# A hybrid decoder layer on one core: split gates in four chunks, and a bank of its own for each product of the second in-projection

## The chip, the cores and the metric

The kernel runs on one core of one Trainium2 chip. The metric is device microseconds (us) of one execution. Five engines matter: TensorE (PE: matmuls; PEld is its weight load), VectorE (DVE), ScalarE (ACT), GpSimd (POOL) and SyncE (SP), which issues most transfers. Results of matmuls land in PSUM, which this program divides into eight banks of 128 partitions x 512 fp32 numbers, and ACT or VectorE carries them from there to SBUF.

## The reference

One layer of a decoder over 2048 positions with 1024 features, all in float32:

```python
h = rms_norm(x, norm1_g)
z = h @ w_in                                   # 1024 -> 2*1024 + 3*512
lru_x, lru_gate, sc_b, sc_c, sc_x = split(z)
lru_x = causal_dwconv(lru_x, lru_conv_w) + lru_conv_b
y_lru = rg_lru(lru_x, ...) * gelu(lru_gate)
y_sc = sc_b * causal_dwconv(sc_c * sc_x, sc_conv_w)
x = x + concat(y_lru, y_sc) @ w_out            # 1536 -> 1024
h = rms_norm(x, norm2_g)
gate, up = split(causal_dwconv(h @ w_up, ffn_conv_w))
x = x + (gelu(gate) * up) @ w_down             # 3072 -> 1024
return rms_norm(x, final_g)
```

`rg_lru` is a gated linear recurrence over positions. Its two gates are `sigmoid(lru_x @ wa + ba)` and `sigmoid(lru_x @ wx + bx)`, where `wa` and `wx` hold 16 blocks of 64x64 on the diagonal. From the gates come a decay `a` and an input `b`, and `h[t] = a[t] h[t-1] + b[t]`.

## The kernel before

Features lie on the partitions, positions along the free axis. The 2048 positions are worked on in two halves of T = 1024, and a half in two blocks of NB = 512, one PSUM bank each. A matmul in the fast form reads operands that are rounded (fp32r). To keep the accuracy of fp32, each operand is split in a high part (ACT copies and rounds, line 239) and a low part (VectorE subtracts, line 240), and a product is made of three matmuls: high x high, high x low, low x high. Where operands are left in plain fp32, one matmul is written, which the trace shows as two records.

The stages follow each other on PE: the in-projection of the first half (0 to about 290 us, `in_phase`), the out-projection of the first half (to about 440), the in-projection of the second half (`in_blocks`, to about 742), its out-projection (to about 860), then the two halves of the ConvFFN.

*First in-projection.* The operands of x are made chunk by chunk (`x_prep`: xh on ACT, line 463, xl on VectorE, line 464); beside that the squares of x are taken on ACT (line 309) and added up on VectorE in ss_a (line 310). The sum is split into rh_a and rl_a, and PE multiplies both with ones to get the mean (ms_a, line 327). After that come the units one by one: eight chunks L0 to L7 of the recurrence and four of the short convolution. For each L chunk `lru_gates` (line 380) makes four plain fp32 matmuls, two blocks times two row halves of 64 partitions, where the row halves are the two 64x64 blocks of the chunk. gw holds the gate weights, cv the convolved input.

*Second in-projection.* Two output chunks at a time, a pair, are made for both blocks by Strassen's scheme in Winograd's form: seven products in place of eight, of four contraction steps each, 12 matmuls per product. W11, W12, W22 are weights as they are loaded, S1 to S4 sums of them; the sums were made in the first half and stored. There are 14 pairs: L0 to L7, three of kind B (the factor sc_b) and four of kind X. A weight operand wW or wS of 128x512 is loaded by SP in pairs (line 842; the name wr_in8W_8W tells that both belong to pair 8) and split into high and low on ACT and VectorE.

For a pair, PE runs W11, then S2, S3 and W22 in one chain in the same bank (zx). After each of them the bank's running sum is wanted, so ACT copies it to SBUF (line 700) before PE goes on in it. S1 and S4 share the bank zc, and W12 has za; these are added to the copies by VectorE (line 704). A round on PE holds the first products of pair j and the last ones of pair j-1, and between them the gates of an earlier chunk. The first output of a pair is called xlin for kind L, prin for X and sbin for B, the second one soin.

When a pair of kind L is complete, `finish` makes its convolution (line 354 on ACT, line 356 on VectorE, three steps), and a round later come the gates, eight sigmoids on ACT (line 391) and the rest of the recurrence with the scan (line 404). Beside all this, the mean of squares for the next norm is gathered: sx_b is squared on ACT (line 1188) and added to ss_b on VectorE (line 1189).

*What sets the order.* PE, SP and GpSimd work in the order in which the program is written. On ACT and VectorE a scheduler places the instructions; a block under `tc.high_priority(offset=...)` ranks ahead by that offset. Each engine then works strictly in the order placed. Pools limit how far it can go ahead: eight banks, two pages for the loads of weights, six for their parts.

Of the kernel before, what the change touches and what calls it, by code (L numbers as in the profile page):

```python
# [12 lines left out]
P = 128  # L13
# [18 lines left out]
GP = 0  # L32
UPP = 200
CP = 160
LATE = ("11", "22")
HSIDE = 1
LASTA = NLRU - 1
# [62 lines left out]
def block_kernel(  # L100
# [275 lines left out]
    def lru_gates(c, half, cv, gw):  # L376
# [3 lines left out]
                nc.tensor.matmul(ps[t], gw[rows, :], cv[rows, blk(t)], start=True, stop=True)  # L380
        return pss

    def lru_scan(c, half, cv, g, *gates, home=None, sign=1.0):
        n = f"{half}_{c}"
        r, i = (flat(p(f"{x}{n}")) for p, x in zip(home or (act, act), "ri"))
# [105 lines left out]
    def in_phase(half, acc, between):  # L491
# [19 lines left out]
            if k == 2:  # L511
                nc.sync.dma_start(prm, par[:, KC:])
        for k in range(KC):
            x_square(half, k, acc, xs[k])
        for _ in loads[2]:
            pass
        gate_w.append(flat(tmp("gw")).rearrange("p (c k) -> p c k", c=NLRU))
        nc.sync.dma_start(gate_w[0], w_gate.rearrange("c p k -> p c k"))
        parts = mean_split(acc, f"a{half}")
        pair_sums(0, NLRU)  # L520
        rs = inv_rms(acc, f"a{half}", parts)
        nc.gpsimd.tensor_copy(mark, rs[:, 0:1])
        ready.append(True)
        ps_2 = pss[2]
        for k in range(2, KC):
            product_step(ps_2, wcol(wts[2], k), acts[k], False, k == KC - 1)
        sum_step()
        cv = lru_conv(0, half, pss[0], rs)
# [3 lines left out]
        for n, (kind, c) in enumerate(UNITS):  # L532
            nxt = UNITS[n + 1] if n + 1 < len(UNITS) else None
            if kind == "L":
                if len(cur) < 2:
                    cur = (*cur, lru_gate(c, half, in_product(NLRU + c, half, acts), rs))
                cv, g = cur
                ps_n = ps_2 or in_product(first_product(nxt), half, acts)
                ps_2 = None
                ps_g = in_product(NLRU + nxt[1], half, acts) if n == 0 else None  # L540
                gates = lru_gates(c, half, cv, gate_w[0][:, c, :])
                if nxt[0] == "L":
                    cur = (lru_conv(nxt[1], half, ps_n, rs),)
                    if ps_g is not None:
                        cur = (*cur, lru_gate(nxt[1], half, ps_g, rs))
                y = lru_scan(c, half, cv, g, *gates)
            else:
                y = sc_second(c, half, acts, rs, sc_first(c, half, acts, rs, ps_n))
                if nxt is not None:
                    ps_n = in_product(first_product(nxt), half, acts)  # L550
                    if nxt[0] == "L":
                        cur = (lru_conv(nxt[1], half, ps_n, rs),)
            keep_y(half, n, y, (4, 8) if n >= NOUT - 2 else (7, 7))
            between(n)
# [123 lines left out]
    class Pair:  # L678
# [17 lines left out]
                    )  # L696

        def copy(self, dst):
            with tc.high_priority(offset=HP):
                nc.scalar.activation(dst, self.x, AF.Copy)  # L700

        def add(self, dst, ps):
            with tc.high_priority(offset=HP):
                nc.vector.tensor_tensor(dst, ps, dst, ALU.add)

        def spread(self):
# [125 lines left out]
    def in_weights(ops):  # L832
# [11 lines left out]
        for at, (i, op) in enumerate(ops):  # L844
            home = vpage if early else raw_tile
            t = home(f"w{op}_in{i}")
            split(t[:, 0, :], t[:, 1, :], raw[:, at, :])
            out.append((t[:, 0, :], t[:, 1, :]))
        return out

# [3 lines left out]
    class InPair(Pair):  # L854
# [5 lines left out]
        def open(self):  # L860
# [7 lines left out]
            else:  # L868
                self.first = flat(vpage(f"sb{n}"))
                self.g = halves(self.first, 0)  # L870

        def first_term(self):
            self.begin()

        def second_term(self):
            self.second()

        def third_term(self):
            self.sum1()

        def fourth_term(self):
            self.run(self.x, "S2", "T2", False, False)
            self.copy(self.g[1])

        def fifth_term(self):
            self.run(self.x, "S3", "T3", False, False)
            self.open_second()
            self.copy(self.n[1])
            self.add(self.n[1], self.c)

        def sixth_term(self):
            self.end()

        def seventh_term(self):
            self.fourth()

        def open_second(self):
            self.other = flat(vpage(f"so{self.name}"))
# [498 lines left out]
```

## Time and profile before

| | us |
|---|---|
| median of 3 runs (2258.54 to 2259.25) | 2259.07 |
| the profiled execution | 2254.52 |
| its span in the trace | 2252.5 |

The granted clock of the profiled execution is 0.998 of full speed. The trace is of one execution of its own; its span goes from the first instruction to the last. The page gives busy times per engine, the idle time of each engine with what ended it (the releaser), and a chain followed back from the last instruction. An engine that waits for another is named in the list of waits as "PE zxin L689 <- ACT soin L700": PE's instruction that writes zxin, at line 689, waited for ACT's instruction that writes soin, at line 700.

### The profile page before, as it was taken

To read this page: it belongs to the slowest core of one execution; us is meant where nothing else is said; L and a number is where in the kernel's file an instruction comes from. 1 tells how busy PE (TensorE), PEld (TensorE's weight loads), DVE (VectorE), ACT (ScalarE), POOL (GpSimd) and SP (SyncE) were. 2 spreads that over 40 slices of the span, in tenths; PEclk is the share of its full clock that TensorE was granted. 3 is DMA by queue.
4 is the path that set the end of the run, shared out by engine and by line. 5 is a ranking of instruction groups with operands and counts; after the bars stand their busy time and mean duration, and the time that the engine had idled before them with its cause. 6 is when DMAs were issued, how large, how long until landed. Compare 5 with 4: busy or idle time off the path is not lost.

```text
span 2252.5 us, 26402 instructions
## 1 busy us (share of the span) xinstructions
PE 2223.2 (99%) x9754; PEld 1815.1 (81%) x9754; DVE 1780.7 (79%) x2062; ACT 1216.2 (54%) x1411; POOL 175.7 (8%) x302
## 2 busy tenths in 40 slices
PE   9999999999999899999999999999999999999997
PEld 7887788887767688888888788888888888888886
DVE  8767879847778899898887887676988888886556
ACT  7538835557797554555544454444544444453343
POOL 0021110000000000110111100000000000000000
PEclk9999999999999999999999999999999999999999
DMA  8486369734434874565557477674223232359754
GB/s 313 104 236 187 121 227 303 273 108 136 164 121 128 311 267 169 180 195 173 166 164 222 128 254 243 232 254 137 99 100 111 98 113 90 108 196 346 243 193 156
DMA packets 157953, 415.01 MB, mean 184 GB/s; under 512 B 16640, under 2 KB 19328, under 8 KB 157248
## 3 DMA queue, kind: packets, MB, share of 16 engines
q1 hardware_dynamic: 135872, 354.86, 45.5%
q0 software_dynamic: 21808, 58.47, 10.1%
q8 instruction: 76, 1.25, 0.2%
q14 instruction: 53, 0.43, 0.1%
q10 hardware_dynamic: 144, 0.00, 0.0%
HBM read 311.55 MB, written 139.46 MB: 200 GB/s over the span
## 4 chain that ended last, share of the span: by engine, by line
PE 85%; issue 5%; ACT 4%; DVE 3%; DMA 2%; POOL 0%; SPq 0%; DVEq 0%; ACTq 0%; POOLq 0%
PE zx L689 21%; PE zin_b L295 13%; PE dx L1022 12%; PE zc L689 11%; PE dy L1022 9%; PE ox L1022 5%; PE za L689 5%; PE oy L1022 4%; PE zxin L689 2%; PE zS L689 1%; PE zcin L689 1%; PE zr_b L380 1%; PE zW L689 1%; PE zain L689 1%; ACT wS_in L239 0%
## 5 line engine op out<-in xcount | busy, mean ns | idle before, releaser
L239 ACT ACTIVATE fh_d<-wrf_d 128x1024 fp32r<-128x1024 f32 x84 | 89.0, 1060 | 204.3 <-PE dy L1022 78.4
L240 DVE TENSOR_TENSOR fl_d<-wrf_d,fh_d 128x1024 fp32r<-128x1024 f32 x84 | 102.7, 1223 | 120.7 <-ACT fh_d L239 118.4
L1022 PE MATMUL dx<-fh_d,wl_d 128*128 128x512 f32 x384 | 149.4, 389 | 0.0
L1022 PE MATMUL dx<-fh_d,wh_d 128*128 128x512 f32 x384 | 149.4, 389 | 0.0
L1022 PE MATMUL dx<-fl_d,wh_d 128*128 128x512 f32 x384 | 149.4, 389 | 0.0
L295 PE MATMUL zin_b<-xh,wh_in 128*128 128x512 f32 x448 | 139.4, 392 | 0.2
L295 PE MATMUL zin_b<-xl,wh_in 128*128 128x512 f32 x448 | 138.2, 389 | 0.1
L295 PE MATMUL zin_b<-xh,wl_in 128*128 128x512 f32 x448 | 137.9, 389 | 0.0
L240 DVE TENSOR_TENSOR wla_up<-wra_up,wha_up 128x1024 fp32r<-128x1024 f32 x48 | 58.8, 1224 | 98.3 <-ACT wha_up L239 98.3
L356 DVE SCALAR_TENSOR_TENSOR cg<-ug,prm,cg 128x1024 f32<-128x1024 f32 x96 | 122.8, 1279 | 8.1 <-ACT cg L352 7.3
L356 DVE SCALAR_TENSOR_TENSOR cu<-un,prm,cu 128x1024 f32<-128x1024 f32 x96 | 122.7, 1278 | 4.7 <-ACT cu L352 4.3
L689 PE MATMUL zc<-hhB,whd_up 128*128 128x512 f32 x368 | 120.8, 389 | 0.0
L689 PE MATMUL zx<-ht,whc_up 128*128 128x512 f32 x368 | 113.4, 389 | 0.0
L1022 PE MATMUL dy<-fh_d,wh_d 128*128 128x512 f32 x288 | 112.0, 389 | 0.0
L1022 PE MATMUL dy<-fl_d,wh_d 128*128 128x512 f32 x288 | 112.0, 389 | 0.0
L1022 PE MATMUL dy<-fh_d,wl_d 128*128 128x512 f32 x288 | 112.0, 389 | 0.0
L240 DVE TENSOR_TENSOR wl_d<-wrw_d,wh_d 128x1024 fp32r<-128x1024 f32 x84 | 102.3, 1218 | 8.3 <-ACT wh_d L239 7.0
L700 ACT ACTIVATE ug<-zx 128x512 f32<-128x512 f32 x92 | 54.8, 596 | 98.1 <-PE zx L689 93.1
L295 PEld LDWEIGHTS zin_b<-xh,wh_in 128*128 128x128 f32 x448 | 83.5, 188 | 23.7 <-issue 3.8
L295 PEld LDWEIGHTS zin_b<-xl,wh_in 128*128 128x128 f32 x448 | 84.1, 188 | 18.1 <-DVE xl L464 0.6
L295 PEld LDWEIGHTS zin_b<-xh,wl_in 128*128 128x128 f32 x448 | 84.1, 188 | 17.4
L239 ACT ACTIVATE wh_d<-wrw_d 128x1024 fp32r<-128x1024 f32 x84 | 87.8, 1046 | 11.6 <-PE zc L689 4.0
(552 smaller groups left out, 6332.2 us busy)
## 6 DMA issues: line engine op xcount, KB each, us to landing
wrc_up<-in_w_up SPq DMA_DIRECT2D x48, 512.0 KB, 4.9
f_d_T<-cg SPq DMA_DIRECT2D x96, 256.0 KB, 2.5
wrw_d<-sd_d_S SPq DMA_DIRECT2D x48, 512.0 KB, 4.6
wrf_d<-f_d_T SPq DMA_DIRECT2D x48, 512.0 KB, 4.2
f_d_B<-cu SPq DMA_DIRECT2D x72, 256.0 KB, 2.4
wrw_d<-in_w_down SPq DMA_DIRECT2D x36, 512.0 KB, 4.8
wrf_d<-f_d_B SPq DMA_DIRECT2D x36, 512.0 KB, 3.3
wr_in<-in_w_in SPq DMA_DIRECT2D x25, 512.0 KB, 5.9
```

Of the source, the lines that this page charges most:

```text
L239: nc.scalar.activation(r32(hi), src, AF.Copy)
L240: nc.vector.tensor_tensor(r32(lo), src, hi, ALU.subtract)
L295: nc.tensor.matmul(ps[t], r32(a), r32(b[:, blk(t)]), start=(first and i == 0), stop=(last and i == 2))
L356: nc.vector.scalar_tensor_tensor(dst, src[:, k : k + T], col(o_w + k), dst, ALU.mult, ALU.add)
L380: nc.tensor.matmul(ps[t], gw[rows, :], cv[rows, blk(t)], start=True, stop=True)
L689: nc.tensor.matmul(ps, r32(p[:, s]), r32(self.hs[k][x][o]), start=f and i == 0, stop=l and i == 2, skip_group_check=True,)
L700: nc.scalar.activation(dst, self.x, AF.Copy)
L1022: nc.tensor.matmul(ps[m], r32(p), r32(x[:, k, :]), start=first and i == 0 and n == 0, stop=(last or not on_x) and i == ni - 1 and n == 2, ...
```

## The change

There are three groups of edits. First, for chunks 2 to 5 of the first half the gates are made of split operands: cv is split in ch and cl, the gate weights of these four chunks are split once, and three products take the place of the one in fp32. This makes 12 matmuls of 64 rows in place of four. Second, in the second in-projection only W11 is still copied by ACT; W12, S2, S3 and W22 each get a bank of their own, and VectorE adds each to the sum in SBUF. The final values are the same sums in another order of work. Third, ranks: the copy of W11 gets 200 (was 120), the squares of x are raised by 20, the splits of weights in `in_weights` by 100. MK is 0, so that loop makes nothing.

```diff
--- before.py
+++ after.py
@@ -32,6 +32,15 @@
 GP = 0
 UPP = 200
 CP = 160
+MK = 0
+XP = 200
+AP = 120
+QP = 20
+IWQ = 100
+APART = ("S2", "S3", "W22")
+LAST_X = "W11"
+GQ = 60
+PARTS = (2, 3, 4, 5)
 LATE = ("11", "22")
 HSIDE = 1
 LASTA = NLRU - 1
@@ -380,6 +389,30 @@
                 nc.tensor.matmul(ps[t], gw[rows, :], cv[rows, blk(t)], start=True, stop=True)
         return pss
 
+    def lru_gates_of_parts(c, half, cv, gw):
+        pss = [pst2(f"z{name}{half}_{c}") for name in "ri"]
+        hi, lo = (flat(act(f"c{x}{half}_{c}")) for x in "hl")
+        with tc.high_priority(offset=GQ):
+            split(hi, lo, cv)
+        for i, (a, b) in enumerate(((gw[0], hi), (gw[0], lo), (gw[1], hi))):
+            for t in range(T // NB):
+                for ps, rows in zip(pss, HALVES):
+                    nc.tensor.matmul(ps[t], r32(a[rows, :]), r32(b[rows, blk(t)]), start=i == 0, stop=i == 2)
+        return pss
+
+    gate_parts = []
+
+    def gates_of(c, half, cv):
+        if c not in PARTS:
+            return lru_gates(c, half, cv, gate_w[0][:, c, :])
+        if not gate_parts:
+            n = max(PARTS) + 1 - min(PARTS)
+            t = flat(tmp("gp"))
+            for i in range(2):
+                gate_parts.append(t[:, i * n * P // 1 : (i + 1) * n * P].rearrange("p (c k) -> p c k", c=n))
+            split(*gate_parts, gate_w[0][:, min(PARTS) : max(PARTS) + 1, :])
+        return lru_gates_of_parts(c, half, cv, [g[:, c - min(PARTS), :] for g in gate_parts])
+
     def lru_scan(c, half, cv, g, *gates, home=None, sign=1.0):
         n = f"{half}_{c}"
         r, i = (flat(p(f"{x}{n}")) for p, x in zip(home or (act, act), "ri"))
@@ -511,18 +544,21 @@
             if k == 2:
                 nc.sync.dma_start(prm, par[:, KC:])
         for k in range(KC):
-            x_square(half, k, acc, xs[k])
+            with tc.high_priority(offset=QP):
+                x_square(half, k, acc, xs[k])
         for _ in loads[2]:
             pass
         gate_w.append(flat(tmp("gw")).rearrange("p (c k) -> p c k", c=NLRU))
         nc.sync.dma_start(gate_w[0], w_gate.rearrange("c p k -> p c k"))
+        ps_2 = pss[2]
+        for k in range(2, 2 + MK):
+            product_step(ps_2, wcol(wts[2], k), acts[k], False, k == KC - 1)
         parts = mean_split(acc, f"a{half}")
         pair_sums(0, NLRU)
         rs = inv_rms(acc, f"a{half}", parts)
         nc.gpsimd.tensor_copy(mark, rs[:, 0:1])
         ready.append(True)
-        ps_2 = pss[2]
-        for k in range(2, KC):
+        for k in range(2 + MK, KC):
             product_step(ps_2, wcol(wts[2], k), acts[k], False, k == KC - 1)
         sum_step()
         cv = lru_conv(0, half, pss[0], rs)
@@ -538,7 +574,7 @@
                 ps_n = ps_2 or in_product(first_product(nxt), half, acts)
                 ps_2 = None
                 ps_g = in_product(NLRU + nxt[1], half, acts) if n == 0 else None
-                gates = lru_gates(c, half, cv, gate_w[0][:, c, :])
+                gates = gates_of(c, half, cv)
                 if nxt[0] == "L":
                     cur = (lru_conv(nxt[1], half, ps_n, rs),)
                     if ps_g is not None:
@@ -696,11 +732,11 @@
                     )
 
         def copy(self, dst):
-            with tc.high_priority(offset=HP):
+            with tc.high_priority(offset=XP):
                 nc.scalar.activation(dst, self.x, AF.Copy)
 
         def add(self, dst, ps):
-            with tc.high_priority(offset=HP):
+            with tc.high_priority(offset=AP):
                 nc.vector.tensor_tensor(dst, ps, dst, ALU.add)
 
         def spread(self):
@@ -844,7 +880,8 @@
         for at, (i, op) in enumerate(ops):
             home = vpage if early else raw_tile
             t = home(f"w{op}_in{i}")
-            split(t[:, 0, :], t[:, 1, :], raw[:, at, :])
+            with tc.high_priority(offset=IWQ):
+                split(t[:, 0, :], t[:, 1, :], raw[:, at, :])
             out.append((t[:, 0, :], t[:, 1, :]))
         return out
 
@@ -869,30 +906,47 @@
                 self.first = flat(vpage(f"sb{n}"))
                 self.g = halves(self.first, 0)
 
+        def part(self, w, x, dst, src):
+            if w in APART:
+                ps = pst(f"z{w}{self.name}")
+                self.run(ps, w, x, True, True)
+                self.sum(dst, ps, src)
+            else:
+                self.run(self.x, w, x, False, w == LAST_X)
+                self.copy(dst)
+
+        def sum(self, dst, ps, src):
+            with tc.high_priority(offset=AP):
+                nc.vector.tensor_tensor(dst, ps, src, ALU.add)
+
         def first_term(self):
-            self.begin()
+            self.open()
+            self.x = pst(f"zx{self.name}")
+            self.run(self.x, "W11", "B11", True, LAST_X == "W11")
+            self.copy(self.g[1])
 
         def second_term(self):
-            self.second()
+            a = pst(f"za{self.name}")
+            self.run(a, "W12", "B21", True, True)
+            self.sum(self.g[0], a, self.g[1])
 
         def third_term(self):
             self.sum1()
 
         def fourth_term(self):
-            self.run(self.x, "S2", "T2", False, False)
-            self.copy(self.g[1])
+            self.part("S2", "T2", self.g[1], self.g[1])
 
         def fifth_term(self):
-            self.run(self.x, "S3", "T3", False, False)
             self.open_second()
-            self.copy(self.n[1])
-            self.add(self.n[1], self.c)
+            self.part("S3", "T3", self.n[0], self.g[1])
+            self.sum(self.n[1], self.c, self.n[0])
 
         def sixth_term(self):
             self.end()
 
         def seventh_term(self):
-            self.fourth()
+            self.part("W22", "T4", self.n[0], self.n[0])
+            self.second_done()
 
         def open_second(self):
             self.other = flat(vpage(f"so{self.name}"))
```

On PE the order of the products stays as it was; bank names and the gates of the four chunks differ. SP and GpSimd have the same orders. ACT and VectorE are placed anew. Lines of the changed program are shifted: 239 and 240 become 248 and 249, 354 and 356 become 363 and 365, 700 becomes 736, 704 becomes 740, 1188 and 1189 become 1242 and 1243; line 920 is the new sum.

The first place is in the eighth round of the second in-projection, on ACT. The rows are in order of work; those of line 700 are copies of a bank, wW_in<-wr_in8W_8W are the high parts of W11 and W12 of pair 8, xlin belongs to the pair before it. Before:

```order
L700 ACTIVATE soin<-zxin 128x512
L407 ACT_TABLE_LOAD
L407 ACTIVATE soin<-soin 128x1024
L700 ACTIVATE xlin<-zxin 128x512
L1188 ACTIVATE sx_b<-sx_b 128x1024
L239 ACTIVATE wW_in<-wr_in8W_8W 128x512
L354 ACTIVATE cv<-xlin,prm 128x1024
L239 ACTIVATE wW_in<-wr_in8W_8W 128x512
L239 ACTIVATE wW_in<-wr_in7W_8S 128x512
L239 ACTIVATE wS_in<-wr_in7W_8S 128x512
```

and with the change:

```order
L736 ACTIVATE xlin<-zxin 128x512
L433 ACT_TABLE_LOAD
L433 ACTIVATE cv<-cv 128x1024
L440 ACT_TABLE_LOAD
L440 ACTIVATE soin<-soin 128x1024
L363 ACTIVATE cv<-xlin,prm 128x1024
L1242 ACTIVATE sx_b<-sx_b 128x1024
L248 ACTIVATE wW_in<-wr_in8W_8W 128x512
L248 ACTIVATE wW_in<-wr_in8W_8W 128x512
L248 ACTIVATE wW_in<-wr_in7W_8S 128x512
L248 ACTIVATE wS_in<-wr_in7W_8S 128x512
```

The two splits of pair 8 stood one ahead of the conv (cv<-xlin) and one behind it; both now stand behind the conv and behind the square of sx_b.

The second place is the same round on VectorE. xlin<-zcin is the sum that completes the first output of the pair before, cv<-xlin are steps of its conv, and wW_in<-wr_in8W_8W are the low parts. Before:

```order
L945 SCALAR_TENSOR_TENSOR soin<-soin,soin 128x512
L562 TENSOR_TENSOR yc<-soin 128x512
L567 TENSOR_TENSOR sbin<-soin,sbin 128x512
L568 SCALAR_TENSOR_TENSOR yc<-yc,soin 128x512
L342 COPY xlin<-xl_halo 128x3
L569 SCALAR_TENSOR_TENSOR yc<-yc,soin 128x512
L704 TENSOR_TENSOR xlin<-zcin,xlin 128x512
L1189 TENSOR_TENSOR ss_b<-ss_b,sx_b 128x1024
L240 TENSOR_TENSOR wW_in<-wr_in8W_8W,wW_in 128x512
L356 SCALAR_TENSOR_TENSOR cv<-xlin,prm,cv 128x1024
L240 TENSOR_TENSOR wW_in<-wr_in8W_8W,wW_in 128x512
```

and with the change:

```order
L920 TENSOR_TENSOR soin<-zW22in,soin 128x512
L437 SCALAR_TENSOR_TENSOR r<-a,h_last,i 128x1024
L604 SCALAR_TENSOR_TENSOR yc<-yc,soin 128x512
L442 TENSOR_TENSOR soin<-soin,r 128x1024
L920 TENSOR_TENSOR xlin<-zS2in,xlin 128x512
L598 TENSOR_TENSOR yc<-soin 128x512
L605 SCALAR_TENSOR_TENSOR yc<-yc,soin 128x512
L740 TENSOR_TENSOR xlin<-zcin,xlin 128x512
L351 COPY xlin<-xl_halo 128x3
L365 SCALAR_TENSOR_TENSOR cv<-xlin,prm,cv 128x1024
L1243 TENSOR_TENSOR ss_b<-ss_b,sx_b 128x1024
L249 TENSOR_TENSOR wW_in<-wr_in8W_8W,wW_in 128x512
```

Two sums of line 920 (of zW22 and zS2) have come into this stretch, the scan (r<-a) has moved behind the first of them, and the low part of W11 stands behind a step of the conv and the sum ss_b.

The third place is the start of the program on VectorE. xl are the low parts of x, wl_in those of the first weights, ss_a<-ss_a,sq_a the sums of squares, sa and sb sums of weights for the second half, rl_a the low part of the sum of squares. Before:

```order
L464 SCALAR_TENSOR_TENSOR xl<-x,g,xh 128x1024
L310 TENSOR_TENSOR ss_a<-ss_a,sq_a 128x1024
L464 SCALAR_TENSOR_TENSOR xl<-x,g,xh 128x1024
L240 TENSOR_TENSOR wl_in<-wr,wh_in 128x256 x2
L283 TENSOR_TENSOR sa<-wr 128x512
L240 TENSOR_TENSOR wl_in<-wr,wh_in 128x256
L283 TENSOR_TENSOR sa<-wr,wr 128x512
L283 TENSOR_TENSOR sb<-wr,sa 128x512
L310 TENSOR_TENSOR ss_a<-ss_a,sq_a 128x1024
L283 TENSOR_TENSOR sb<-wr,sb 128x512
L240 TENSOR_TENSOR rl_a<-ss_a,rh_a 128x1024
```

and with the change:

```order
L497 SCALAR_TENSOR_TENSOR xl<-x,g,xh 128x1024
L319 TENSOR_TENSOR ss_a<-ss_a,sq_a 128x1024
L319 TENSOR_TENSOR ss_a<-ss_a,sq_a 128x1024
L249 TENSOR_TENSOR wl_in<-wr,wh_in 128x256 x3
L497 SCALAR_TENSOR_TENSOR xl<-x,g,xh 128x1024
L249 TENSOR_TENSOR rl_a<-ss_a,rh_a 128x1024
L292 TENSOR_TENSOR sa<-wr 128x512
L292 TENSOR_TENSOR sa<-wr,wr 128x512
L292 TENSOR_TENSOR sb<-wr,sa 128x512
L292 TENSOR_TENSOR sb<-wr,sb 128x512
```

The last sum of squares has moved ahead of the last low part of x, and rl_a follows that directly; the sums of weights come after it.

## The prediction

> **What bounds the kernel now.** I read the page first: how busy each engine is, then the chain that ended last.
>
> ```profile
> span 2252.5 us, 26402 instructions
> PE 2223.2 (99%) x9754; PEld 1815.1 (81%) x9754; DVE 1780.7 (79%) x2062; ACT 1216.2 (54%) x1411; POOL 175.7 (8%) x302
> PE 85%; issue 5%; ACT 4%; DVE 3%; DMA 2%; POOL 0%; SPq 0%; DVEq 0%; ACTq 0%; POOLq 0%
> ```
>
> PE is the bound: 2223.2 of 2252.5 us. So the change can gain in two ways only: fewer PE steps, or fewer PE waits. The second view lists PE's waits: who waits, for whom, the total in us, how often, and the longest.
>
> ```profile
> PE oy L1022 <- DVE fl_o L240: 2.5, 1, 2.5
> PE zxin L689 <- ACT soin L700: 2.3, 3, 0.8
> PE zcin L689 <- DVE soin L704: 1.9, 1, 1.9
> PE ox L1022 <- DVE fl_o L240: 1.9, 1, 1.9
> PE zxin L689 <- ACT sbin L700: 1.5, 1, 1.5
> PE zx L689 <- ACT ug L700: 1.4, 1, 1.4
> PE zxin L689 <- ACT xlin L700: 1.4, 2, 1.0
> PE ms_a L327 <- ACT rh_a L239: 1.1, 1, 1.1
> PE ms_a L327 <- DVE rl_a L240: 0.5, 1, 0.5
> PE zxin L689 <- ACT prin L700: 0.4, 1, 0.4
> PE zxin L689 <- DVE wW_in L240: 0.4, 1, 0.4
> ```
>
> All rows that name zxin or zcin lie in the second in-projection. Seven waits are for an ACT copy (line 700): 2.3 + 1.5 + 1.4 + 0.4 = 5.6 us. One is for a split of weights (line 240), one for VectorE's sum of the last pair. What the other engines do there is in the stretches of that stage:
>
> ```profile
> 560.00:640.00 80.00, 77.44 (x333) 59.16 (x332) 60.51 (x74) 65.55 (x88) 3.91 (x8) 1.00 0.46 154
> 640.00:742.00 102.00, 96.47 (x415) 74.64 (x414) 80.87 (x96) 86.35 (x113) 8.62 (x16) 1.00 0.47 154
> ```
>
> Columns: length, then busy us of PE, PEld, DVE, ACT and POOL. ACT is busier than VectorE in both (86.35 against 80.87 us of 102), at the full clock (1.00). One wait in detail, PE's rows and then ACT's:
>
> ```profile
> 638.22 0.39 PE L689 MATMUL zxin<-hhT1x,wS_in 128*128 128x512 f32 x1
> ...
> 643.66 0.39 PE L689 MATMUL zcin<-hhT1x,wS_in 128*128 128x512 f32 x1
> 645.57 0.50 PE L689 MATMUL zxin<-hhB11x,wS_in 128*128 128x512 f32 x1 [1.52 <-ACT sbin L700]
> 645.91 0.40 PE L689 MATMUL zxin<-hlB11x,wS_in 128*128 128x512 f32 x1
> ...
> 644.22 0.68 ACT L391 ACTIVATE i<-zi_b,prm 64x512 f32<-64x512 f32 x1
> 644.92 0.60 ACT L700 ACTIVATE sbin<-zxin 128x512 f32<-128x512 f32 x1
> ```
>
> The S2 product ended with the matmul of 638.22, but its copy stands behind eight sigmoids on ACT, the last of them at 644.22. S3 goes on in the same bank, so PE stands after S1 (643.66) until the copy is done. It costs more than its gap. Unhindered, matmuls follow each other at
>
> ```profile
> 601.23 0.39 PE L689 MATMUL zxin<-hhB11x,wS_in 128*128 128x512 f32 x1
> ...
> 601.91 0.39 PE L689 MATMUL zxin<-hhB11x,wW_in 128*128 128x512 f32 x1
> ```
>
> three steps in 0.68 us, 0.227 us each. From 643.66 to 645.91 are 2.25 us for two steps that take 0.45: 1.80 us lost for a gap of 1.52. I therefore add 0.28 us to each gap.
>
> **The change part by part.** *Gates of chunks 2 to 5, first half.* Before, one block of a chunk stands in the trace so:
>
> ```profile
> 53.51 0.69 PE L380 MATMUL zr_b<-cv,gw 64*128 64x512 f32 x1
> 53.51 0.69 PE L380 MATMUL zi_b<-cv,gw 64*128 64x512 f32 x1
> 54.04 0.59 PE L380 MATMUL zr_b<-cv,gw 64*128 64x512 f32 x1
> 54.47 0.59 PE L380 MATMUL zr_b<-cv,gw 64*128 64x512 f32 x1
> 54.90 0.59 PE L380 MATMUL zr_b<-cv,gw 64*128 64x512 f32 x1
> 55.42 0.73 PE L295 MATMUL zin_b<-xh,wh_in 128*128 128x512 f32 x2
> ```
>
> The two row halves start together, in four steps of 0.53, 0.43, 0.43 and 0.52 us: 1.91 us, of which 4 x 0.43 = 1.72 is the stream and 0.19 the change of shape. Afterwards it is three products of two blocks, six pairs. The trace shows no 64-row matmul of split operands. Side by side, as the fp32 ones run, at 0.227 a pair they take 1.36 us, 0.36 less: **-1.4 us** for four chunks. One after the other they would take 12 x 0.227 = 2.72 us, 1.0 more: +4.0. I take the first, since the pair in these rows starts at one time; +4.0 stays as an end. Nothing suggests pairs faster than 0.227. The four extra splits of 128x1024 lie on ACT and VectorE, which in the first 290 us are busy for 196 and 227 us; a gate block comes more than a product (2.72 us for 12 matmuls of 128x512) after its conv, which covers them. Without that cover the price would be one VectorE piece of 1.2 us each.
>
> *The start.* The waits for rh_a and rl_a give 1.1 + 0.5 + 2 x 0.28 = 2.2 us. The squares and their sums now come earlier, so both should go. What is late next is the last low part of x:
>
> ```profile
> 26.14 1.28 DVE L464 SCALAR_TENSOR_TENSOR xl<-x,g,xh 128x1024 fp32r<-128x1024 f32 x1
> 27.34 0.75 DVE L240 TENSOR_TENSOR wl_in<-wr,wh_in 128x256 fp32r<-128x256 f32 x2
> 30.15 1.22 DVE L310 TENSOR_TENSOR ss_a<-ss_a,sq_a 128x1024 f32<-128x1024 f32 x1
> ...
> 28.98 0.62 PE L295 MATMUL zin_b<-xl,wh_in 128*128 128x512 f32 x2
> ```
>
> It started at 26.14; now the last sum of squares (about 1.14 us to the next start) and three pieces of wl_in (0.34 each) go ahead: 26.14 + 1.14 + 1.02 + 1.2 = 29.5 to 29.6. PE wants it at 28.98, so a new wait of 0.6 + 0.28 = 0.9. Net **-1.3 us**, between 0 and -2.2.
>
> *Second in-projection.* Three copies per pair leave ACT (0.60 us in the row of 644.92); three adds come to VectorE (0.68 in the rows below, 0.60 to the next start). Each product but W11 has its own bank, so S2, S3 and W22 no longer wait for a reader: the seven waits go, **-7.6 us** (5.6 + 7 x 0.28). A bank comes back some 28 matmuls or more later in the written order (over 6 us), and its reader needs 0.6 us once its turn comes; I take no cost there.
>
> The adds do lengthen VectorE's queue, however, and the scheduler moved the weights' splits behind other work. The place is the eighth round:
>
> ```profile
> 594.44 1.05 ACT L1188 ACTIVATE sx_b<-sx_b 128x1024 f32<-128x1024 f32 x1
> 595.39 0.62 ACT L239 ACTIVATE wW_in<-wr_in8W_8W 128x512 fp32r<-128x512 f32 x1
> 600.37 1.25 ACT L354 ACTIVATE cv<-xlin,prm 128x1024 f32<-128x1024 f32 x1 [4.36 <-DVE xlin L704]
> ...
> 599.65 0.68 DVE L704 TENSOR_TENSOR xlin<-zcin,xlin 128x512 f32<-128x512 f32 x1
> 600.25 1.22 DVE L1189 TENSOR_TENSOR ss_b<-ss_b,sx_b 128x1024 f32<-128x1024 f32 x1
> 601.38 0.68 DVE L240 TENSOR_TENSOR wW_in<-wr_in8W_8W,wW_in 128x512 fp32r<-128x512 f32 x1
> ```
>
> Before, ACT split W11 of pair 8 at 595.39, ahead of the conv at 600.37; PE reads it first at 601.91. In the changed order ACT's split stands behind the conv and sx_b, and VectorE's behind the xlin add, one step of the conv and ss_b. Two more adds, of W22 and S2 (1.2 us), stand ahead of the xlin add, and the scan, now behind the first of them, begins some 0.5 later: the xlin add ends near 602.0 instead of 600.3. Then conv 1.15, sx_b 0.95, ss_b 1.15 and the low part 0.65 follow each other: 602.1 + 3.9 = 606.0. PE comes to its third matmul at 601.91 + 0.45, less the 0.7 of the wait saved at 590, plus 2.05 of the round below: 603.7. Wait 2.3 to 2.4, with its 0.28 **+2.7 us**. In round 6 the same order is seen, with two steps of the conv ahead of the low part: the add ends 0.9 later, 558.8; conv 1.15, two steps of 1.2 and the low part 0.65 give 563.2 with the start-up. PE would go on at 560.6; the cost is 2.75 instead of 0.4 + 0.28, **+2.05**. That is bounded by 0 (adds hidden, as W11's high part is behind nothing) and by a whole chain of 3.9 in each.
>
> [...]
>
> *The end of the stage.* VectorE's last sum, the 1.9 us row, stands behind splits for the out-projection. It gets three adds more and PE comes earlier; I take nothing, between 0 and -2.2. The waits for fl_o at the out-projection (2.5 and 1.9) hang on VectorE and on stores behind the last scan; ACT reaches the last sigmoids earlier by roughly what PE gains, so I leave them as they are.
>
> Sum: -1.4 - 1.3 - 7.6 + 2.7 + 2.05 = **-5.6 us**. The profiled execution took 2254.52, 2.0 more than its span and 4.6 less than the median of the runs shown, 2259.07; I take the difference off the median: **2253.5 us**.
>
> **The rivals.** *A, nothing replaces the copies' waits.* VectorE has a fifth of the stage's later stretch free (80.87 busy of 102), so the splits could still be in time, and the start and the end of the stage lose their waits too: -1.4 - 2.2 - 7.6 - 0.7 and half of the end's 2.2 make -13, **2246**. For it: seven waits of the list have one cause, which is gone. Against: the order at round 8. [...]
>
> *B, given back.* The stage's end hangs on VectorE, not on PE: cv of the last chunk, its scan, the stores and fl_o. Then of the 2.85 us that the second in-projection gains, the waits of 1.9 and 2.5 grow by as much, and the first half alone stays, -2.7 or less if the splits cost 1 to 2 us more: -3 to 0, **2257**. For it: VectorE gets 13 pairs x 3 adds x 0.6 = 23 us more in some 300. Against: it has idle time in both stretches quoted (20 and 21 us).
>
> *C, slower.* One mechanism: the split of the next W11 stands behind the add of a pair in every one of the six L rounds from L2 on, not in two. From the point where the add ends when PE wants the weights, each round costs the whole chain of 3.9 + 0.28 = 4.2: 6 x 4.2 = 25, less the gains of 1.4 + 1.3 + 7.6 = 10.3: +15, **2274**. It ends over 0.2% slower from (10.3 + 4.5) / 6 = 2.5 us a round. Against it: round 4 has some 5 us of margin in the written order.
>
> *D, the gates don't overlap.* The +4.0 in place of -1.4: -0.2, **2259**.
>
> **How the numbers follow.** The forecast 0.41, A 0.16, B 0.28, C 0.08, D 0.07. A measurement of this kernel tells about 0.2%, 4.5 us, from no change. Faster by more than that: the forecast, which lies 1.1 us beyond the bound, and A: 0.57. Within: B and D, 0.35. Slower: 0.08. The range takes in A and D: 2246 to 2260.5.
>
> **What would show it.** Right: no row of PE waiting for a copy of S2, S3 or W22; two waits for wW_in of 2 to 3 us near 560 and 603; gate blocks of chunks 2 to 5 with 0.23 us steps and both halves starting together; no wait at ms_a, and one of about 0.6 at the last xl. Wrong: gate steps that alternate between the halves (D); no wait for wW_in (A); PE's start of the out-projection unmoved, or fl_o's waits longer (B); waits for wW_in in most L rounds (C). The forecast fails most likely in the xlin adds' ends, which I walked by hand: each us that they come earlier takes up to 1 us off in both rounds.

## The result, and the profile after

The changed kernel takes 2268.55 us (median, 2265.91 to 2270.47), the one before 2258.91 (2258.54 to 2259.25): a ratio of 1.0043, 95% interval 1.0029 to 1.0058. It is slower; the forecast was 2253.5 and the range ended at 2260.5. The profiled execution took 2268.78, at a granted clock of 0.993 (0.998 before). First the page of the changed kernel:

```profile
span 2267.0 us, 26497 instructions
PE 2232.0 (98%) x9770; PEld 1823.4 (80%) x9770; DVE 1809.9 (80%) x2106; ACT 1199.3 (53%) x1376; POOL 176.5 (8%) x302
PE 79%; DVE 6%; issue 5%; ACT 5%; DMA 3%; POOL 1%; SPq 0%; DVEq 0%; POOLq 0%; ACTq 0%
```

PE is busy 9 us longer and the span is 14.4 us longer. In the chain that ended last, PE's share fell from 85% to 79%. Its list of waits (who waits, for whom, total, times, longest, in us):

```profile
PE zr_b L400 <- DVE cl L249: 3.7, 3, 1.5
PE zr_b L400 <- ACT ch L248: 2.7, 2, 1.4
PE zxin L725 <- ACT wW_in L248: 2.6, 2, 1.3
PE zx L725 <- ACT ug L736: 2.4, 2, 1.4
PE oy L1076 <- DVE fl_o L249: 2.3, 2, 1.2
PE ox L1076 <- DVE fl_o L249: 2.3, 1, 2.3
PE zr_b L389 <- DVE cv L365: 2.2, 1, 2.2
PE zxin L725 <- DVE wW_in L249: 1.9, 2, 1.0
```

All seven waits for copies are gone, and so are those for ms_a. The two for wW_in came as forecast. New are the first two rows, five waits for ch and cl, the split operands of the gates, and the wait for cv at the last gates. The loss can be placed by the starts of PE's steps in the two traces:

| PE starts | before | after | difference |
|---|---|---|---|
| gates of chunk 0 | 53.51 | 51.71 | -1.8 |
| second in-projection | 447.04 | 457.78 | +10.7 |
| gates after round 6 | 569.09 | 583.71 | +14.6 |
| gates after round 8 | 610.16 | 628.17 | +18.0 |
| gates of the last round but one | 699.95 | 711.66 | +11.7 |
| up-projection's first product | 862.00 | 875.15 | +13.2 |
| first down-projection (dx) | 1322.32 | 1336.75 | +14.4 |

The first half gives away 12.5 us between the first gates and its end. The second in-projection loses some 7 us up to round 8 and wins 6.3 of them back. At the splits of chunk 2 the changed kernel's trace shows ACT, then VectorE, then PE (start, duration, engine and line, operation, and in brackets the idle time before and what ended it):

```profile
142.22 0.63 ACT L248 ACTIVATE gp<-gw 128x512 fp32r<-128x512 f32 x1 [14.23 <-DMA y_d_T<-yc]
...
146.68 1.25 ACT L363 ACTIVATE cv<-xl,prm 128x1024 f32<-128x1024 f32 x1 [1.93 <-DVE xl L464]
153.17 1.06 ACT L248 ACTIVATE wh_in<-wr_in 128x1024 fp32r<-128x1024 f32 x1 [5.25 <-DMA wr_in<-in_w_in]
154.14 1.04 ACT L248 ACTIVATE ch<-cv 128x1024 fp32r<-128x1024 f32 x1
```
```profile
142.89 0.69 DVE L249 TENSOR_TENSOR gp<-gw,gp 128x512 fp32r<-128x512 f32 x1 [9.57 <-ACT gp L248]
...
156.22 1.22 DVE L249 TENSOR_TENSOR cl<-cv,ch 128x1024 fp32r<-128x1024 f32 x1
```
```profile
155.23 0.50 PE L400 MATMUL zr_b<-ch,gp 64*128 64x512 f32 x1 [1.25 <-ACT ch L248]
...
157.49 0.50 PE L400 MATMUL zr_b<-cl,gp 64*128 64x512 f32 x1 [1.52 <-DVE cl L249]
...
159.02 1.22 PE L304 MATMUL zin_b<-xh,wh_in 128*128 128x512 f32 x2
```

ACT stands idle for 14.23 us ahead of the split of the gate weights: the page for gp is given back only when the store of yc has landed. VectorE stands for 9.57 us with it, and the conv comes later: its last step ends at 153.97, in the kernel before at 149.47. Then ch stands behind wh_in, which waits 5.25 us for a load, as it did in the kernel before (5.73 us). At this chunk, none of it is an engine with too much to do. In the last PE row, the two records last 1.22 us instead of the 0.73 of the same form before. The reason is seen in windows of the same trace (columns: length, then busy us of PE, PEld, DVE, ACT and POOL, then the granted clock):

```profile
154.66:158.07 3.41, 1.32 (x10) 0.79 (x12) 2.77 (x3) 2.86 (x3) 0.00 (x0) 1.00 1.01 147
158.07:161.48 3.41, 3.41 (x12) 2.27 (x9) 0.00 (x0) 0.00 (x0) 0.00 (x0) 0.50 0.91 267
571.09:574.50 3.41, 1.10 (x4) 0.61 (x5) 3.37 (x4) 2.78 (x5) 0.08 (x1) 1.00 0.78 290
574.50:577.91 3.41, 3.41 (x10) 2.67 (x9) 3.41 (x6) 0.00 (x0) 0.00 (x0) 0.50 0.56 131
```

In this trace, after each window in which PE stood for 2.1 to 2.4 us, the granted clock is 0.50 for the next 3.41 us. Before the kernel's tail (its last 10 us) the changed profile has six such spells, the one at 209.27 two windows long; that of before has none. Its nearest case is the wait of 2.5 us for fl_o, in the kernel before:

```profile
763.01:766.43 3.42, 1.85 (x9) 1.19 (x7) 3.42 (x5) 1.86 (x2) 0.00 (x0) 1.00 0.39 159
766.43:769.84 3.41, 2.48 (x11) 2.06 (x12) 3.41 (x6) 0.00 (x0) 1.48 (x3) 1.00 0.82 273
```

The border of the window falls into that wait: 1.57 us on one side, 0.94 on the other, and the clock stays at 1.00.

### The profile page after: what moved, and what is told of

Read it like the earlier page. It is cut to its first block, busy times and chain, and to the rows that moved or that the text cites. A ratio compares the mean times of both kernels' runs of the same rounds, so it can differ in the third digit from the quotient of the medians.

```text
span 2267.0 us, 26497 instructions
## 1 busy us (share of the span) xinstructions
PE 2232.0 (98%) x9770; PEld 1823.4 (80%) x9770; DVE 1809.9 (80%) x2106; ACT 1199.3 (53%) x1376; POOL 176.5 (8%) x302
## 4 chain that ended last, share of the span: by engine, by line
PE 79%; DVE 6%; issue 5%; ACT 5%; DMA 3%; POOL 1%; SPq 0%; DVEq 0%; POOLq 0%; ACTq 0%
PE zx L725 20%; PE dx L1076 12%; PE zc L725 10%; PE dy L1076 9%; PE ox L1076 5%; PE za L725 5%; PE zin_b L304 4%; PE oy L1076 4%; PE zcin L725 2%; PE zxin L725 2%; PE zain L725 1%; PE zS2in L725 1%; PE zW22in L725 1%; PE zS3in L725 1%; DMA wrc_up<-in_w_up 1%
```

## The experiments

Each was timed beside the kernel before on its own chip; ratios are to that kernel.

### Which part costs: the gates alone, and all but the gates

```diff
-PARTS = (2, 3, 4, 5)
+PARTS = ()
```

> The change without its split gates (all gates in plain fp32). Theory: the split gates cost 12.5 us of the first half (the step between the gates of chunk 1 and the second in-projection), because gp, ch and cl come late on ScalarE and VectorE and PE stands, and because the clock is halved behind two of these waits. Then this takes 2256 us, 12 less than the change, and PE shows no wait ahead of the first half's gates. Rival, the banks and adds of the second in-projection are what costs: then it stays at 2264 us or more.

2258.68 us, ratio 0.9998 (0.9988 to 1.0007). From the start of the second in-projection to its last gates PE is a constant 11.3 us ahead of the changed kernel, and 11.2 at the end. The other way round, the gates' edit alone in the kernel before:

```diff
+GQ = 60
+PARTS = (2, 3, 4, 5)
...
-                gates = lru_gates(c, half, cv, gate_w[0][:, c, :])
+                gates = gates_of(c, half, cv)
```

> The kernel before with the split gates alone. Theory: 2268 us, 9 to 12 more than before, with gp waiting for a page in ScalarE's queue and waits for ch and cl at the gates of chunks 2, 4 and 5. Rival, the split gates gain by themselves and lose only beside the new ranks: 2255 to 2258 us.

2271.18 us, ratio 1.0055 (1.0039 to 1.0071); PE waits 3.4 us for ch and 3.1 for cl. So the split gates are the loss, with or without the rest, and the rest alone changes nothing that can be measured.

### Whose fault the late splits are

First the moment of gp: its split at the gates of chunk 0.

```diff
-        if c not in PARTS:
-            return lru_gates(c, half, cv, gate_w[0][:, c, :])
         if not gate_parts:
...
+        if c not in PARTS:
+            return lru_gates(c, half, cv, gate_w[0][:, c, :])
```

> The change with the gate weights' split (gp) written at the gates of chunk 0 in place of chunk 2, where a page is free earlier. Theory: in the change, gp waits 14 us in ScalarE's queue for a page that a store of y holds, and the x squares, the weights' split and the conv of chunk 2 come 4 us late behind it; so the waits at the gates of chunk 2 (1.25 and 1.52 us) and the half clock behind them go, 4 to 5 us of the 11; those at chunks 4 and 5 stay. 2263 to 2265 us. Rival: ch and cl are late for themselves at all chunks; then the waits at chunk 2 stay and the time is within 1.5 us of the change.

2271.1 us, ratio 1.0055 (1.0037 to 1.0073), no gain where 4 to 5 us were expected; the longest wait for ch grew to 3.4. gp keeps a tmp page for as long as it is read, so now another tile waits for the store of yc. VectorE in this kernel:

```profile
145.17 0.69 DVE L603 TENSOR_TENSOR yd<-sv,sv 128x512 f32<-128x512 f32 x1 [10.92 <-DMA y_d_T<-yc]
```

So an earlier moment doesn't help; by this row there is one page too few. Next, more cover: the gates of these chunks one product later.

```diff
-                ps_g = in_product(NLRU + nxt[1], half, acts) if n == 0 else None
+                ps_g = in_product(NLRU + nxt[1], half, acts) if n == 0 or c in PARTS else None
```

> The change with the gates of chunks 2 to 5 one product of 48 matmuls (10.9 us) later on PE, as chunk 0 has them already. Theory: ch and cl come too late by less than 3 us each, so all waits at these gates go, and their half clocks; the first half then takes 11 us less than in the change and some 0.2 to 0.36 a chunk less than with fp32 gates: 2257 us. Rival: the page of gp still holds up ScalarE, and PE waits for the weights or the conv instead; 2263 us or more.

2277.2 us, ratio 1.0084 (1.0069 to 1.0099). PE's list of waits begins

```profile
PE zr_b L400 <- ACT ch L248: 6.9, 1, 6.9
PE zin_b L304 <- DVE g L464: 4.1, 3, 3.1
```

More cover doesn't help here. The same with a third page for weight loads:

```diff
-NW = 2
+NW = 3
```

> The change with the later gates of chunks 2 to 5 and with three pages for the loads of weights. If both mends add up: 2254 us, 1 us less than three pages without split gates. Rival: the page of gp costs what the split gates gain; 2256 to 2260.

2273.46 us, ratio 1.0071 (1.0056 to 1.0086): a little better, still far from before. Now the page itself: gp from another pool, act in place of tmp.

```diff
-            t = flat(tmp("gp"))
+            t = flat(act("gp"))
```

> The change with the page of gp taken from the 28 pages of the pool act in place of the 7 of tmp; ScalarE's order stays but for gp and two neighbouring rows, VectorE's too. Where gp was split earlier (e5), VectorE stood 10.9 us for a page all the same, for yd: gp keeps one of the seven pages for its whole life. Theory: the missing page delays the x squares, the conv of chunk 2 and SyncE's next load of weights by 4 to 8 us; with it back, PE shows no wait at the gates of chunk 2, and those at chunks 4 and 5, where ch stands behind eight sigmoids, an exp and a tanh, stay or grow by 1 us. 2262 to 2265 us. Rival: ScalarE's wait for the load of weights is what holds ch, whatever the page: waits at chunk 2 as before, 2267 us or more.

2269.44 us, ratio 1.0039 (1.0024 to 1.0054). The waits at chunk 2 are gone, those at chunks 4 and 5 have grown. VectorE's row at chunk 4 in this kernel:

```profile
205.60 1.23 DVE L249 TENSOR_TENSOR cl<-cv,ch 128x1024 fp32r<-128x1024 f32 x1 [3.24 <-DMA si_d<-sb]
```

Its source ch was ready at 202.93 (ACT's split began at 201.87 and took 1.06). What ended the wait is a store of sb, a sum of weights: an act page comes back when it lands. Late gates on top of it (the edit of ps_g again), and late gates with the third page for loads:

> As e9, and the gates of chunks 2 to 5 one product later on PE. Theory: with the page back, the 10.9 us more that ch and cl have are enough at all four chunks: no waits there, a block of split gates takes 0.2 us less than one in fp32, and the time is that of the change without split gates or up to 1 us less: 2257 to 2259. Rival: the later gates hold up what follows (the convs, the evacuations of g), as in e6 at 201 and 287 us: 2262 or more.

> As e10, with three pages for the loads of weights: the two mends together. If they add up 2254 to 2256 us, otherwise as e10.

2277.89 (1.0074, 1.0059 to 1.0089) and 2272.65 us (1.0054, 1.0037 to 1.0071). Neither helps; in both, VectorE's cl still comes up to 2.9 us late at a gate. Last, ch and cl from the pool of the weights' parts as well:

```diff
-        hi, lo = (flat(act(f"c{x}{half}_{c}")) for x in "hl")
+        hi, lo = (flat(wv_page(f"c{x}{half}_{c}", "v")) for x in "hl")
...
-            t = flat(tmp("gp"))
+            t = flat(act("gp"))
```

> The change with gp on a page of act, as in e9, and ch and cl on pages of the pool v (weights' parts, given back by PE) in place of act (28 pages, given back by the stores of sa and sb). In e9 ScalarE stood for a store of sa ahead of ch and VectorE 2.9 and 3.2 us for a store of sb ahead of cl. Theory: the pages are what the split gates wait for. Then no instruction that writes ch or cl waits for a store, ch of chunk 2 follows its conv at once, the waits at the gates of chunks 2 to 5 fall from 8 us to under 3 with their half clocks, and the time to 2260 us or less. Rival: ch is late by ScalarE's sigmoids at chunks 3 to 5 in any case, and the pages taken from the weights hold up those: 2266 us or more.

2261.0 us, ratio 1.0003 (0.9993 to 1.0013), 8 us below the run with gp alone moved. PE has no wait for ch or cl. The split stands right behind its conv on ACT, and a block of PE at chunk 3 runs unhindered:

```profile
146.01 1.06 ACT L248 ACTIVATE ch<-cv 128x1024 fp32r<-128x1024 f32 x1 [5.13 <-DVE cv L365]
```
```profile
177.42 0.49 PE L400 MATMUL zr_b<-ch,gp 64*128 64x512 f32 x1
177.43 0.49 PE L400 MATMUL zi_b<-ch,gp 64*128 64x512 f32 x1
...
179.01 0.73 PE L304 MATMUL zin_b<-xh,wh_in 128*128 128x512 f32 x2
```

From 177.42 to 179.01 are 1.59 us; in fp32 the block took 1.91. Both halves start together. With these pages the split gates cost next to nothing, so the pools that they take from make the loss. Besides the 14.23 us for gp, one wait for such a page can be seen in the changed kernel itself, VectorE's at chunk 5:

```profile
235.96 1.23 DVE L249 TENSOR_TENSOR cl<-cv,ch 128x1024 fp32r<-128x1024 f32 x1 [2.95 <-DMA si_d<-sa]
```

At chunk 4 no page shows there: ch starts at 206.46, and ACT has been busy since 194.90 with the conv, eight sigmoids and two more activations. With the new pages the scheduler also placed ch ahead of the second of these two. How much of the cure at chunk 4 is the page and how much is the place on ACT isn't separated. The split gates gain nothing either, for 4 x 0.32 = 1.3 us is spent on new waits (1.06 us for g near 275). Two more that start from this kernel, one with late gates, one with GQ = 1000 and NW = 3:

> As e12, with the gates of chunks 2 to 5 one product later on PE. If pages were the whole cause, all waits at these gates go and the four blocks take 0.2 us less each than in fp32: 2257 us. Rival: the later gates hold up the following chunk's conv and the evacuation of g, as in e6 and e10, where PE waited for g at 287 us and for sigmoids at 260: 2262 or more.

> As e12, with the split of cv ranked highest (it then stands among the sigmoids, ahead of the exp), and with three pages for the loads of weights in the second half. If the first half then costs no more than without split gates: 2255 us; each us over that is what the split gates still wait.

2264.45 (1.0028, 1.0011 to 1.0044) and 2260.5 us (1.0009, 0.9996 to 1.0022). In the first, PE waits 3.7 us for g; in the second 0.9 for gp, 1.8 for g and 1.5 for xl. Neither finds a gain in split gates. The second, with three pages for loads, is by its ratio even 6 us over the run with three pages and no split gates (0.9982, below). In the traces 4.5 us of that lie ahead of the second in-projection, which starts at 449.63 and there at 445.17. So it is in the run with the moved pages alone that the split gates cost next to nothing.

### What the half clock costs

Five idle products of 128x512, whose results are overwritten, at two gates and at two of the W11, so that PE doesn't stand:

```diff
+FILL = {2: 5, 4: 5}
+FILL_IN = {6: 5, 8: 5}
...
+        for i in range(FILL.get(c, 0)):
+            nc.tensor.matmul(pss[i % 2][i // 2 % 2], ones_r, r32(spare[0][:, blk(0)]), start=True, stop=True)
...
+            for _ in range(FILL_IN.get(self.at(), 0)):
+                nc.tensor.matmul(self.x, ones_r, r32(self.hs[0]["B11"][0]), start=True, stop=True)
```

> The change with five idle products of 128x512 (never used, overwritten by the next start) ahead of the gates of chunks 2 and 4 and ahead of W11 of pairs 6 and 8, where PE stands anyway: PE waits less within a window, and nothing comes later that wasn't late. Theory, the clock is halved after a window of 3.4 us in which PE stood over about 2 us: the four windows fall to some 1.0 to 1.3 us of idleness, the granted clock stays 1.00 there, and the time falls by 5 x 1.7 = 8 us to about 2260. Rival, the slow matmuls come from something else, such as transfers: the 20 products cost nothing or up to 20 x 0.227 = 4.5 us, and the time is 2268 to 2273.

2269.67 us, ratio 1.0047 (1.0032 to 1.0062). None of the four places is halved. But on ACT the scheduler placed ch of chunk 3 behind a split of weights, a square of x and an activation with its table load (178.32 to 182.59, without idle time), which made a wait of 4.6 us with 10.24 us at half clock around it. So the order on ACT can make such a wait too, without a page. What the half clock costs, that run doesn't settle. A smaller one: no split gates, and two idle products at pair 8 only.

```diff
-PARTS = (2, 3, 4, 5)
+FILL_IN = {8: 2}
...
+PARTS = ()
...
+            for _ in range(FILL_IN.get(PAIRS.index((self.kind, self.c)), 0)):
+                nc.tensor.matmul(self.x, ones_r, r32(self.hs[0]["B11"][0]), start=True, stop=True)
```

> The change without its split gates, and with two idle products of 128x512 ahead of W11 of pair 8, where PE stands for 1.23 us; VectorE's and ScalarE's orders are the same but for one neighbouring pair of rows after it. Theory: the window of 3.4 us there holds 2.05 us of idleness and halves the clock; with 0.45 less it doesn't: the stretch from the end of S3 before W11 of pair 8 to the next gates, 12.8 us in the kernel without split gates, takes 11.1. Rival, the slow matmuls are not from the idleness: 12.8 again, or 0.45 more. The median moves by less than can be told, the profile decides.

2258.29 us, ratio 0.9999 (0.9989 to 1.0009). The products at pair 8 decided nothing, but round 6, where the two kernels have the same instructions and the same two waits, gave the answer by chance. PE and the windows without the fill (all but the gates):

```profile
559.29 0.39 PE L725 MATMUL zS3in<-hhB11x,wS_in 128*128 128x512 f32 x1
561.01 0.50 PE L725 MATMUL zxin<-hhB11x,wW_in 128*128 128x512 f32 x1 [1.33 <-ACT wW_in L248]
...
562.79 0.50 PE L725 MATMUL zxin<-hhB11x,wW_in 128*128 128x512 f32 x1 [1.05 <-DVE wW_in L249]
```
```profile
560.15:563.57 3.42, 1.51 (x5) 0.97 (x6) 3.38 (x5) 2.37 (x5) 0.00 (x0) 1.00 0.65 242
563.57:566.98 3.41, 3.41 (x9) 2.67 (x8) 3.41 (x5) 0.15 (x1) 0.00 (x0) 0.50 0.66 159
```

and with it:

```profile
558.20 0.39 PE L729 MATMUL zS3in<-hhB11x,wS_in 128*128 128x512 f32 x1
559.92 0.50 PE L729 MATMUL zxin<-hhB11x,wW_in 128*128 128x512 f32 x1 [1.33 <-ACT wW_in L250]
```
```profile
557.41:560.82 3.41, 1.91 (x8) 0.93 (x6) 2.35 (x2) 3.41 (x6) 1.32 (x3) 1.00 0.96 352
560.82:564.24 3.42, 2.55 (x11) 2.13 (x12) 3.42 (x6) 0.61 (x2) 0.00 (x0) 1.00 0.38 98
564.24:567.65 3.41, 3.41 (x17) 2.83 (x16) 3.30 (x5) 1.87 (x3) 0.00 (x0) 1.00 0.94 332
```

In the first both waits fall into one window, with 1.91 us of standing, and the next has half the clock. In the second a border lies between them (1.50 and 0.87 us) and the clock stays. From the last S3 matmul to the next gates PE takes 559.29 to 572.36 = 13.07 us in the first, 558.20 to 569.62 = 11.42 in the second. One window at half clock cost 1.65 us here, about half its length of 3.41 us. Yet the gates after round 8 start at 616.87 and 616.81. With the fill PE came 2.74 us ahead out of round 6 (569.62 against 572.36). Of that, 0.45 went into the two idle products, 1.1 into a longer wait for ACT's split (2.34 us for 1.23), and another 1.1 into half clock, which lasted two windows there (605.20 to 612.02) instead of one.

### Earlier weights

All but the gates, with three pages for weight loads and five for their parts, in place of two and six:

```diff
-NW = 2
+NW = 3
...
-PARTS = (2, 3, 4, 5)
+PARTS = ()
```

> The change without its split gates and with three pages in place of two for the loads of weights (of ten, so one less for other pages); ScalarE's first split of pair 8 then stands ahead of the conv again. Theory, the waits at W11 of pairs 6 and 8 come from the order of the splits: at least the one at pair 8 goes, with its half clock, 3 to 4 us each; 2249 to 2253 us. Rival, the splits are late by the adds that stand on VectorE ahead of them in any order: within 1 us of the kernel without split gates.

2255.53 us (2251.42 to 2258.91), ratio 0.9982 (0.9973 to 0.9991): faster than both kernels. The waits for wW_in are gone. At the mean of squares ahead of the last two gates (ms_b) PE is 8.9 us ahead of before (681.87 against 690.79), at the up-projection 2.55 (859.45 against 862.00). Between them its list of waits in this kernel has

```profile
PE zcin L725 <- ACT i L424: 3.0, 1, 3.0
PE zr_b L389 <- DVE cv L365: 2.9, 2, 2.1
```

and two windows at half clock lie behind them (after the 3.0 us the matmuls follow each other at 0.43 us from 735.95 to 738.93, where unhindered ones take 0.227). So most of the gain is given back where ACT's sigmoids and VectorE's conv end the stage. No run gives the kernel before a third page, so how much of the rest belongs to the banks stays open.

## Why the prediction was wrong

**The step that failed** is the price of the split gates, -1.4 us. Its matmuls were right: both halves start together, and an unhindered block takes 1.59 us, 0.32 less than in fp32 (forecast 0.36). What failed is "a gate block comes more than a product (2.72 us for 12 matmuls of 128x512) after its conv, which covers them", with "one VectorE piece of 1.2 us each" as the price without cover. It asked whether ACT and VectorE have time, not whether gp, ch and cl have pages. The time was there: in the profile of before, the gates of chunks 2 to 5 start 6.2 to 13.3 us after their conv's last step. But the new tiles take pages that come back only when stores land. Behind the 14.23 us for gp the conv of chunk 2 ends 4.5 us later, and PE came to the gates before ch and cl were made. The sum now: five waits, 3.7 + 2.7 = 6.4 us; with 0.28 for each gap 7.8; three windows at half clock in the first half (the one from 158.07 and the two from 209.27), 3 x 1.65 = 5.0; less 4 x 0.32 = 1.3. That is 11.5, against 11.3 measured at the second in-projection between the two traces with and without the edit (10.7 at the gates of chunk 6). The range had no such end: for the gates its worst was D, +4.0 for matmuls one after the other, and that mechanism didn't occur.

**The start** was right: -1.8 at the first gates for -1.3; with all but the gates it is -1.65, where PE waits 0.3 us for the last xl, forecast 0.6.

**The copies** went as said. In the stretch between the gates after round 8 and those at 700 us, nearly free of other changes, PE takes 711.66 - 628.17 = 83.5 us, before 699.95 - 610.16 = 89.8. Five of the seven waits lie there, 4.5 us and with 0.28 each 5.9; 6.3 were won.

**The waits for W11** came in the two rounds named, of nearly the size named. Round 6 of the changed kernel, ACT's row and PE's two:

```profile
571.69 1.14 ACT L248 ACTIVATE wW_in<-wr_in6W_6W 128x512 fp32r<-128x512 f32 x2
```
```profile
572.36 0.50 PE L725 MATMUL zxin<-hhB11x,wW_in 128*128 128x512 f32 x1 [1.33 <-ACT wW_in L248]
...
574.14 0.94 PE L725 MATMUL zxin<-hhB11x,wW_in 128*128 128x512 f32 x2 [1.05 <-DVE wW_in L249]
```

PE was to lose 2.75 (by the forecast's own 563.2 and 560.6 it would be 2.6 + 0.28 = 2.9, a slip of 0.1); the gaps are 1.33 + 1.05 and, with what surrounds them, some 2.8. In round 8 they add up to some 2.5 for 2.7. Rival C, a wait in every round, is out. The missing term is the clock: each pair of waits falls into one window (2.3 us of standing in that from 571.09, 2.1 in that from 615.46), the next one has a granted clock of 0.50, and two times 1.65 us follow. From its first product to that of the out-projection, the stage takes 298.0 us in the trace with all but the gates (446.43 to 744.41) and 295.7 before (447.04 to 742.71): +2.3 for a forecast of -2.85. Of the 5.2 between them the two windows are 3.3; a third, behind the last gates, makes up to 1.65 more, partly hidden in later waits. In the out-projection shorter waits for fl_o (2.7 us for 4.5) give 1.6 back.

**The end of the stage**, taken as nothing, was nearly that: the wait of 1.9 for VectorE's last sum became one of 2.2 for the conv. Behind it the clock is halved (0.50 from 748.58 to 751.99). When the waits for W11 are taken away as well, most of the gain is given back there, as rival B had it, though at the last gates rather than at fl_o.

**What the trace of before didn't say.** The profiled execution had no halved window before the tail, and its 2254.52 us is the shortest time on record for that kernel, 4.6 under the median of 2259.07. The clock explains little of the 4.6: twenty other executions at the same granted clock, 0.998, took 2256.18 to 2261.56. The rest stayed open. The traces' difference, 14.4 us, is larger than that of the medians, 9.6, and all but the gates is 3.2 us behind in the traces and even in the medians. The whole 3.2 arises in the up-projection and its waits: at its first product the two traces are 0.07 us apart (862.07 and 862.00). There PE waits for ug (3.4 us with all but the gates, 1.4 before, 2.4 in the changed kernel), with a window at half clock from 1259.88. The edit of `copy` raised the rank of these copies too, from 120 to 200, but in the up-projection ACT's order differs in two places only, and neither is beside these waits. At the first of them the chain leads back to a load: VectorE's sum of weights waits for wrc_up until 1211.23, before until 1210.29. Why that load lands later, and where the rest comes from, stayed open.

## What to carry to other kernels

Before an operand is split or staged, ask not only which engine has time for it, but whose page it takes and what gives that page back: a page that a store held left ACT idle for 14.23 us here. Price a wait of PE with the window it falls into: in round 6 two waits of 1.33 and 1.05 us in one window cost 1.65 us more (13.07 us against 11.42) than with the border of a window between them. And a stretch in which ACT or VectorE ends last gives back much of what PE wins, as the last gates did with three pages (8.9 us ahead became 2.55); look there first for what a removed wait is worth.

## What the runs showed of the hardware

In the changed profile the halved spells lie on a grid of 3.413 us: they begin at 158.07, 209.27 and 574.50, which are 15 and 107 windows apart (51.20 and 365.23 us), and one window lasts from 158.07 to 161.48. The kernel's steps drift across this grid from run to run, as in round 6 above: the last S3 matmul starts 0.86 us ahead of a border (559.29, 560.15) with all but the gates, and 2.62 us ahead of one (558.20, 560.82) with the two idle products. With all but the gates, 1.91 us of standing in the window from 560.15, in two waits with matmuls between them, was followed by a clock of 0.50; in the kernel before, 1.57 us in that from 763.01 was not. These runs show no sharp limit: with gp on an act page, 1.90 us in the window from 746.30 left the clock at 1.00, and with late gates on the moved pages 1.67 us in that from 606.98 halved it.

Part of the difference between executions goes with the clock: with three load pages, the one execution at a mean clock of 0.998 took 2251.42 us and the five at 0.996 some 2256.5. It isn't the whole: of the run with two idle products, two executions at 0.996 took 2254.22 and 2265.97 us.
